# Order of the two weight halves, the engine of a small copy, and the place of the row sums in a two-layer decoder step

## The chip, the cores and the metric

The kernel runs on one core of one Trainium2 chip. The metric is the device time of one execution in microseconds. Before the change it is 1097.23 us, the median of three runs (1093.21, 1097.23 and 1097.97).

In the profile the engines are PE (TensorE, matmuls), PEld (its weight loads), DVE (VectorE), ACT (ScalarE), POOL (GpSimd) and SP (SyncE, which only issues transfers). L198 is line 198 of the kernel's file.

## What is computed

One inference step of a decoder with two layers: 512 new prompt tokens and 8 decode tokens, model width 1024, feed-forward width 2816, all in float32. Layer 0 mixes tokens by sliding-window attention with rotary positions, layer 1 by gated linear attention (GLA). Behind either stands a gated feed-forward block with a causal convolution of width 3 on its gate branch:

```python
def conv_ffn(x, buf, w_up, conv_w, conv_b, w_down):
    T = x.shape[1]
    h = x @ w_up
    a, u = h[..., :D_FF], h[..., D_FF:]
    ap = jnp.concatenate([buf.astype(a.dtype), a], axis=1)
    c = conv_b + sum(conv_w[j] * ap[:, j:j + T] for j in range(CONV_W))
    y = (jax.nn.gelu(c, approximate=False) * u) @ w_down
    return y, ap[:, T:]

# in each layer i, for the prompt and the decode tokens alike:
x = layer_norm(ALPHA * x + mixer(x), ln_mix_g[i], ln_mix_b[i])
f, conv = conv_ffn(x, buf, ffn_w_up[i], ffn_conv_w[i], ffn_conv_b[i], ffn_w_down[i])
x = layer_norm(ALPHA * x + f, ln_ffn_g[i], ln_ffn_b[i])
```

Outputs are the two activations, the key and value caches, the GLA states and the last two rows of each gate branch (the convolution's state).

## The kernel before

**Layout.** Activations are held transposed: 128 features on the partitions, tokens along the free dimension. The 520 tokens are cut into group a (256 prompt tokens) and group b (256 prompt tokens and the 8 decode tokens). A convolution runs along the free dimension, so group b needs the last two columns of group a: its history, kept in `hist`.

**Products in two parts.** TensorE is fed with `fp32r` values, a rounded float32. To keep accuracy every operand is split into a high part (rounded) and a low part (the rest): `wh`, `wl` for weights, `xh`, `xl` for activations. A product is high by high, high by low and low by high, three matmuls for each 128 by 128 block, all summed in PSUM. In `product` (L228 to L249) the matmuls with `wl` come last for some units (L247, `behind`).

**Weights.** The weights are cut into units of 128 by 1024 float32, 512 KB. Each unit is loaded by SP into one of two raw buffers (`raw`, L193), ScalarE or POOL rounds it into `wh`, and `wl` is made in one of two ways. In the first, VectorE subtracts (L204, L225, L318). In the second, which the program calls `low_by_dma` (L207 to L210), ScalarE writes the negated high part into `wl` and POOL issues a transfer that loads the same weight from HBM again and adds it to `wl` on the way: low = weight - high. The second way is used for the gate, value and down units of the feed-forward blocks, for the first weight block of each pair (below), and for the first units behind three of the four inner LayerNorms (`parts`, L212 to L226, whose operations are put behind chosen instructions of a LayerNorm).

**Stages of a layer.** The mixer and its output projection; the LayerNorm of group a, then that of group b (`ln_chunk`, `ln_end`); then the feed-forward block. Its 22 feature blocks run in two manners. The first four (`PAIRED`) are a gate unit and a value unit each, so eight units, multiplied for group a and group b separately (`ffn_gate`, `ffn_value`): the gate-and-value stage. The other 18 are pairs (`ffn_pair`), which multiply gate and value of both groups together with seven half products in place of eight, in the manner of Strassen and Winograd. For that they need sums and differences of rows of a and b, which `row_sums` (L460) and `row_sum1` (L505) make during the gate-and-value stage, with VectorE and ScalarE. Down projections are mixed in as soon as their inputs are there.

**The convolution's path in the gate-and-value stage** (L801 to L825). A tile `aext` gets two columns of history (zeros for group a, L807; a copy of `hist` for group b, L809) and the gate product behind them (L810). L812 to L814 apply the three taps, L816 saves the history of group a, L818 does the decode tokens with `base`, which POOL has worked out from the convolution's old state (`ffn_base`, L775 to L788: a transfer into `sconv` issued by ScalarE, then L783 to L787). GELU follows (L823), and the value unit's product is multiplied onto it (L831) and split.

**What sets the order.** Every engine and every transfer queue works in order. The program is written as generators: a counter `slot` rises by one with every product of a group, and a piece of work that yields n is taken up again n slots later (`spawn`, `due`). This gives an order of writing; a scheduler with a timeline simulation of its own then sets each engine's final order, with dependencies, the order of writing as priority, and bounds such as `issue_after(x)`, which puts instructions behind x on their engine. `behind_chain` (L790) uses it to put extra work behind the newest GELU and product. The row sums are spawned at the end of group b's LayerNorm (L450) and run in four parts: differences of the first half of the rows (L476, L478), then after 2, 3 and 2 further slots the other sums. The base is spawned 3 slots after the stage opens (L773).

```python
    def low_by_dma(self, l, h, src):
        self.nc.scalar.activation(l, h.bitcast(F32), AF.Copy, scale=-1.0)
        self.nc.gpsimd.dma_start(out=l, in_=src, accum_op=ALU.add)
```

Of the kernel before, what the change touches and what calls it, by code (L numbers as in the profile page):

```python
# [11 lines left out]
F32 = mybir.dt.float32  # L12
F32R = mybir.dt.float32r
I32 = mybir.dt.int32
AF = mybir.ActivationFunctionType
ALU = mybir.AluOpType
# [50 lines left out]
HEAVY = 2, 3, 5  # L67
# [35 lines left out]
class Net:  # L103
# [80 lines left out]
    def load_unit(self, u, pieces=1, late=False):  # L184
        src, nt = self.units[u][0], self.units[u][1]
        nc = self.nc
        if nt == 0:
            return self.load_rank(u)
        r = self.raw.tile([P, KD * P], F32, name="raw")
        h, l = ((self.wx if u == self.extra else self.wts).tile([P, KD * P], F32R, name=name) for name in ("wh", "wl"))  # L190
        n = nt * P // pieces
        for c in (slice(i * n, (i + 1) * n) for i in range(pieces)):
            nc.sync.dma_start(out=r[:, c], in_=src[:, c])  # L193
            if late:
                self.spawn(self.parts(u, h[:, c], l[:, c], r[:, c], src[:, c]), 1)
                continue
            if u >= HIACT:
                nc.scalar.activation(h[:, c], r[:, c], AF.Copy)  # L198
            else:
                nc.gpsimd.tensor_scalar(h[:, c], r[:, c], 1.0, 0.0, op0=ALU.mult, op1=ALU.add)  # L200
            if self.units[u][2] in (self.ffn_down2, self.ffn_gate, self.ffn_value):
                self.low_by_dma(l[:, c], h[:, c], src[:, c])
            else:
                nc.vector.tensor_tensor(l[:, c], r[:, c], h[:, c].bitcast(F32), op=ALU.subtract)  # L204
        self.w[u] = (h, l)

    def low_by_dma(self, l, h, src):  # L207

        self.nc.scalar.activation(l, h.bitcast(F32), AF.Copy, scale=-1.0)  # L209
        self.nc.gpsimd.dma_start(out=l, in_=src, accum_op=ALU.add)  # L210

    def parts(self, u, h, l, r, src):  # L212
# [5 lines left out]
        n = u - norm[4] if norm else 0  # L218
        with behind(norm and (*[norm[1]] * 4, self.square, self.exp)[n]):
            self.nc.scalar.activation(h, r, AF.Copy)  # L220
            if norm and self.phases.index(norm[4] - 1) in HEAVY:
                self.low_by_dma(l, h, src)
                return
# [31 lines left out]
    def pair_tasks(self, u):  # L255
# [13 lines left out]
        def upper():  # L269
# [3 lines left out]
            nc.sync.dma_start(out=r1, in_=src1)  # L273
            h, l = slot()
            nc.scalar.activation(h, r0, AF.Copy)
            self.low_by_dma(l, h, src0)
            keep(h, l, "a11", "a12")
# [99 lines left out]
    def ln_end(self, g, i, last=False):  # L377
# [70 lines left out]
        if i % 2 == 0:  # L448
            if g.i:
                self.spawn(self.row_sums(i), 1)  # L450
            return
# [8 lines left out]
    def row_sums(self, i):  # L460
# [13 lines left out]
        self.t1 = [self.ln.tile([P, NT - 256], F32, name=name, bufs=c)[:, :256] for name, c in (("sq", 2), ("sq", 2), ("mu", 1), ("msq", 1))]  # L474
        with self.tc.issue_after(self.rest):
            v.tensor_tensor(self.t1[0], row(a, 0), row(b, 0), op=ALU.subtract)  # L476
        for k in range(1, half):
            v.tensor_tensor(self.t1[k], row(a, k), row(b, k), op=ALU.subtract)  # L478
        yield 2
        with self.behind_chain():  # L480
# [11 lines left out]
            for k in range(half):  # L492
                v.scalar_tensor_tensor(tl[:, k], even(r)[:, k], -1.0, th[:, k].bitcast(F32), op0=ALU.mult, op1=ALU.subtract)
        yield 3
        with self.behind_chain():
# [305 lines left out]
    def ffn_gate(self, g, u, layer, j, q):  # L801
# [4 lines left out]
        if g.i == 0:  # L806
            nc.gpsimd.memset(a[:, 0:2], 0.0)  # L807
        else:
            self.pcopy(a[:, 0:2], self.hist[:, j])  # L809
        nc.scalar.copy(a[:, 2:2 + n], ps)  # L810
# [715 lines left out]
```

## Time and profile before

| | us |
|---|---|
| median of three runs | 1097.23 |
| the profiled execution | 1098.08 |
| its span, first to last instruction | 1096.1 |
| TensorE busy | 1058.4 (97%) |
| VectorE busy | 866.2 (79%) |
| ScalarE busy | 686.1 (63%) |
| GpSimd busy | 325.8 (30%) |
| granted TensorE clock, mean | 0.994 |

All times within the profile are counted from the start of the span. A row of a timeline has the start, the duration, the engine, the line, the operation, the tiles written and read, and in brackets the idle time of the engine before it with what ended it. The list of waits gives for each waiting line and releaser the total, the number and the longest. The granted clock is the share of full speed that TensorE was given. Transfers appear as issues, with the time from issue to landing.

### The profile page before, as it was taken

The numbers are of one execution on the slowest core, as the hardware profiler recorded it, in microseconds if no ns is written. First come the engines' busy times: TensorE is split into PE (matmuls) and PEld (weight loads), VectorE is DVE, ScalarE is ACT, GpSimd is POOL, SyncE is SP. The second block draws the span as 40 slices with busy tenths as digits, with TensorE's granted clock in tenths as the row PEclk, the third lists the DMA queues.
The fourth block names the chain that finished last, engine by engine and source line by source line (L and its number), as shares of the span: only waits on it lengthen the run. The fifth ranks groups of instructions, "written<-read, shape, count | busy, mean of one in ns | idle before, by whom it ended". The sixth has DMA issues, their size and how long they took to land.

```text
span 1096.1 us, 23852 instructions
## 1 busy us (share of the span) xinstructions
PE 1058.4 (97%) x9174; PEld 1029.8 (94%) x9174; DVE 866.2 (79%) x1812; ACT 686.1 (63%) x1356; POOL 325.8 (30%) x513
## 2 busy tenths in 40 slices
PE   8999999999999999999999999999899999999995
PEld 7998799999999999999999999898899999999995
DVE  7897758987788778978766767687888788778975
ACT  5677657776656665647666756477676656665643
POOL 3476553511111110274231111363311111110263
PEclk9999999999999999999999999999999999999998
DMA  6554139597777774348134455367487777774422
GB/s 228 150 162 136 24 108 226 129 221 183 181 174 175 174 190 117 111 144 220 55 115 157 132 157 172 93 173 209 127 212 187 181 173 177 174 188 117 114 68 79
DMA packets 65473, 167.44 MB, mean 153 GB/s; under 512 B 8104, under 2 KB 28624, under 8 KB 65360
## 3 DMA queue, kind: packets, MB, share of 16 engines
q1 hardware_dynamic: 50960, 119.47, 33.6%
q0 software_dynamic: 12240, 44.57, 23.2%
q10 hardware_dynamic: 2160, 1.89, 0.5%
q8 instruction: 72, 1.18, 0.4%
q14 instruction: 41, 0.34, 0.1%
HBM read 153.24 MB, written 8.47 MB: 148 GB/s over the span
## 4 chain that ended last, share of the span: by engine, by line
PE 76%; DVE 8%; DMA 6%; ACT 4%; POOL 2%; issue 2%; SPq 1%; DVEq 0%; ACTq 0%; POOLq 0%
PE widep L312 9%; PE widep L314 9%; PE widep L313 9%; PE accp L240 8%; PE accp L242 8%; PE accp L244 7%; PE widep L937 5%; PE widep L934 5%; PE widep L936 5%; DMA raw<-in_w_up 2%; PE accp L954 2%; DMA raw<-in_w_qkv 2%; PE onep L314 1%; PE onep L313 1%; PE onep L312 1%
## 5 line engine op out<-in xcount | busy, mean ns | idle before, releaser
L317 ACT ACTIVATE wh<-raw 128x1024 fp32r<-128x1024 f32 x72 | 76.3, 1060 | 96.2 <-PE widep L937 49.9
L198 ACT ACTIVATE wh<-raw 128x1024 fp32r<-128x1024 f32 (+1 forms) x91 | 95.0, 1047 | 40.7 <-PE widep L313 12.4
L313 PE MATMUL widep<-tl,wh 128*128 128x264 f32 (+1 forms) x432 | 119.1, 276 | 0.0
L314 PE MATMUL widep<-th,wl 128*128 128x264 f32 (+1 forms) x432 | 119.1, 276 | 0.0
L312 PE MATMUL widep<-th,wh 128*128 128x264 f32 (+1 forms) x432 | 119.1, 276 | 0.0
L240 PE MATMUL accp<-xh_b,wh 128*128 128x264 f32 x400 | 112.6, 282 | 2.5 <-DVE hprod L831 2.0
L244 PE MATMUL accp<-xh_b,wl 128*128 128x264 f32 x400 | 111.7, 280 | 0.0
L210 POOL DMA_DIRECT2D wl<-in_w_down x28 | 24.3, 866 | 284.2 <-ACT wl L209 273.1
L240 PE MATMUL accp<-xs_a,wh 128*128 128x256 f32 x400 | 105.6, 283 | 2.9 <-ACT wh L198 1.9
L242 PE MATMUL accp<-xl_b,wh 128*128 128x264 f32 x384 | 106.8, 278 | 0.0
L242 PE MATMUL accp<-xs_a,wh 128*128 128x256 f32 x384 | 102.1, 282 | 0.5 <-DVE xs_a L318 0.4
L318 DVE TENSOR_TENSOR wl<-raw,wh 128x1024 fp32r<-128x1024 f32 x72 | 88.1, 1223 | 8.1 <-ACT wh L317 8.1
L209 ACT ACTIVATE wl<-wh 128x1024 fp32r<-128x1024 f32 x85 | 89.3, 1053 | 1.1
L204 DVE TENSOR_TENSOR wl<-raw,wh 128x1024 fp32r<-128x1024 f32 (+2 forms) x63 | 77.9, 1244 | 14.0 <-ACT wh L198 13.4
L312 PEld LDWEIGHTS widep<-th,wh 128*128 128x128 f32 x432 | 82.1, 190 | 0.0
L313 PEld LDWEIGHTS widep<-tl,wh 128*128 128x128 f32 x432 | 82.1, 190 | 0.0
L314 PEld LDWEIGHTS widep<-th,wl 128*128 128x128 f32 x432 | 82.1, 190 | 0.0
L858 DVE TENSOR_TENSOR merged<-widep,conv 128x528 f32<-128x528 f32 x72 | 37.4, 561 | 55.3 <-PE widep L314 55.2
L240 PEld LDWEIGHTS accp<-xs_a,wh 128*128 128x128 f32 x400 | 76.4, 194 | 4.5 <-ACT wh L198 2.5
L312 PE MATMUL widep<-xh_b,wh 128*128 128x264 f32 x288 | 79.6, 276 | 0.0
L313 PE MATMUL widep<-xl_b,wh 128*128 128x264 f32 x288 | 79.5, 276 | 0.0
L314 PE MATMUL widep<-xh_b,wl 128*128 128x264 f32 x288 | 79.5, 276 | 0.0
(426 smaller groups left out, 4048.1 us busy)
## 6 DMA issues: line engine op xcount, KB each, us to landing
raw<-in_w_up SPq DMA_DIRECT2D x88, 512.0 KB, 3.9
wl<-in_w_up POOLq DMA_DIRECT2D x52, 512.0 KB, 6.6
raw<-in_w_down SPq DMA_DIRECT2D x44, 512.0 KB, 3.6
wl<-in_w_down POOLq DMA_DIRECT2D x28, 512.0 KB, 6.4
raw<-in_w_gla SPq DMA_DIRECT2D x24, 512.0 KB, 3.5
raw<-in_w_mix_o SPq DMA_DIRECT2D x16, 512.0 KB, 4.1
qs<-hl SPq DMA_DIRECT2D x64, 64.0 KB, 2.1
sgla<-in_state_gla SPq DMA_DIRECT2D x16, 256.0 KB, 2.7
```

Of the source, the lines that this page charges most:

```text
L198: nc.scalar.activation(h[:, c], r[:, c], AF.Copy)
L204: nc.vector.tensor_tensor(l[:, c], r[:, c], h[:, c].bitcast(F32), op=ALU.subtract)
L209: self.nc.scalar.activation(l, h.bitcast(F32), AF.Copy, scale=-1.0)
L240: nc.tensor.matmul(o, h[:, ks], xh, start=k == 0, stop=False)
L242: nc.tensor.matmul(o, h[:, ks], xl, start=False, stop=False)
L244: nc.tensor.matmul(o, l[:, ks], xh, start=False, stop=not tail and k == nt - 1)
L312: self.nc.tensor.matmul(o, h[:, ks], rh, start=k == 0, stop=False)
L313: self.nc.tensor.matmul(o, h[:, ks], rl, start=False, stop=False)
L314: self.final = self.nc.tensor.matmul(o, l[:, ks], rh, start=False, stop=k == KD // 2 - 1).ins
L317: self.nc.scalar.activation(hi, src, AF.Copy)
L318: self.nc.vector.tensor_tensor(lo, src, hi.bitcast(F32), op=ALU.subtract)
L934: self.final = nc.tensor.matmul(o, l[:, ks], rh, start=False, stop=k == nk - 1).ins
```

## The change

Three edits, all on how and when things are done; what is computed stays the same.

First, where the low part comes by an adding transfer, ScalarE writes the negated value straight from the raw weight (the rounding happens on writing), and this and the transfer stand before the copy that makes the high part. Before, the high part was made first and negated after. The number of operations and transfers is the same.

Second, group b's two columns of history are copied into `aext` by ScalarE in place of POOL.

Third, the row sums are spawned 4 slots after group b's LayerNorm in place of 1; all four first differences now stand behind the newest GELU and product (before, only the first was bound, behind the last low part of the LayerNorm), and the later parts follow after 1, 2 and 2 slots in place of 2, 3 and 2. So the four parts come at slots 4, 5, 7 and 9 in place of 1, 3, 6 and 8.

```diff
             if late:
                 self.spawn(self.parts(u, h[:, c], l[:, c], r[:, c], src[:, c]), 1)
                 continue
+            adding = self.units[u][2] in (self.ffn_down2, self.ffn_gate, self.ffn_value)
+            if adding:
+                self.low_by_dma(l[:, c], r[:, c], src[:, c])
             if u >= HIACT:
                 nc.scalar.activation(h[:, c], r[:, c], AF.Copy)
             else:
                 nc.gpsimd.tensor_scalar(h[:, c], r[:, c], 1.0, 0.0, op0=ALU.mult, op1=ALU.add)
-            if self.units[u][2] in (self.ffn_down2, self.ffn_gate, self.ffn_value):
-                self.low_by_dma(l[:, c], h[:, c], src[:, c])
-            else:
+            if not adding:
                 nc.vector.tensor_tensor(l[:, c], r[:, c], h[:, c].bitcast(F32), op=ALU.subtract)
...
-    def low_by_dma(self, l, h, src):
-
-        self.nc.scalar.activation(l, h.bitcast(F32), AF.Copy, scale=-1.0)
+    def low_by_dma(self, l, r, src):
+
+        self.nc.scalar.activation(l, r, AF.Copy, scale=-1.0)
         self.nc.gpsimd.dma_start(out=l, in_=src, accum_op=ALU.add)
...
         with behind(norm and (*[norm[1]] * 4, self.square, self.exp)[n]):
+            adding = norm and self.phases.index(norm[4] - 1) in HEAVY
+            if adding:
+                self.low_by_dma(l, r, src)
             self.nc.scalar.activation(h, r, AF.Copy)
-            if norm and self.phases.index(norm[4] - 1) in HEAVY:
-                self.low_by_dma(l, h, src)
+            if adding:
                 return
...
             h, l = slot()
+            self.low_by_dma(l, r0, src0)
             nc.scalar.activation(h, r0, AF.Copy)
-            self.low_by_dma(l, h, src0)
             keep(h, l, "a11", "a12")
...
             if g.i:
-                self.spawn(self.row_sums(i), 1)
+                self.spawn(self.row_sums(i), 4)
             return
...
-        with self.tc.issue_after(self.rest):
-            v.tensor_tensor(self.t1[0], row(a, 0), row(b, 0), op=ALU.subtract)
-        for k in range(1, half):
-            v.tensor_tensor(self.t1[k], row(a, k), row(b, k), op=ALU.subtract)
-        yield 2
+        with self.behind_chain():
+            for k in range(half):
+                v.tensor_tensor(self.t1[k], row(a, k), row(b, k), op=ALU.subtract)
+        yield 1
...
-        yield 3
+        yield 2
...
         else:
-            self.pcopy(a[:, 0:2], self.hist[:, j])
+            nc.scalar.copy(a[:, 0:2], self.hist[:, j])
         nc.scalar.copy(a[:, 2:2 + n], ps)
```

## The prediction

> **What bounds the kernel now.** I read the page first, then the waits of TensorE, then the chain of work that ended last, and only then single engines in time.
>
> ```profile
> PE 1058.4 (97%) x9174; PEld 1029.8 (94%) x9174; DVE 866.2 (79%) x1812; ACT 686.1 (63%) x1356; POOL 325.8 (30%) x513
> ```
>
> TensorE is busy for 1058.4 of 1096.1 us, so everything that a change of order can win lies in 38 us of gaps, and only those in the stages that the diff touches count. The waits of TensorE in the two gate-and-value stages (the window 168 to 217 us in the first layer, 739 to 792 us in the second) are these; columns: total, times, longest.
>
> ```profile
> PE accp L240 <- DVE hprod L831: 1.0, 1, 1.0
> PE accp L247 <- DMA wl<-in_w_up: 0.8, 1, 0.8
> PE accp L244 <- DMA wl<-in_w_up: 0.6, 1, 0.6
> PE accp L247 <- DVE xl_b L444: 0.4, 1, 0.4
> ...
> PE accp L244 <- DMA wl<-in_w_up: 3.4, 1, 3.4
> PE accp L247 <- DMA wl<-in_w_up: 1.3, 2, 1.0
> PE accp L240 <- DVE hprod L831: 1.0, 1, 1.0
> PE accp L247 <- DVE xl_b L444: 0.3, 1, 0.3
> ```
>
> That is 2.8 us in the first layer and 6.0 us in the second. The two stages run the same program, yet the second lasts 4 us longer (53 against 49 us), and the waits explain only 3.2 of them. The clock explains the rest (columns: window, us, PE, PEld, DVE, ACT, POOL busy with counts, granted clock, DMA share, GB/s):
>
> ```profile
> 776.90:780.20 3.30, 3.27 (x15) 3.27 (x16) 0.64 (x1) 1.10 (x2) 0.86 (x1) 0.50 0.17 15
> 203.20:206.50 3.30, 3.28 (x29) 3.28 (x30) 3.30 (x8) 2.78 (x5) 1.01 (x1) 1.00 0.00 0
> ```
>
> Right behind the 3.4 us wait the granted clock is 0.50 for 3.3 us: 15 matmuls where the same place of the first layer does 29. The 14 missing ones, at 3.3/29 us each, are 1.6 us. No shorter wait of this trace is followed by it. [...]
>
> What releases the wait at 203.2 us is told by the chain of the first layer (start, us, what):
>
> ```profile
> 169.84 8.80 DMA raw<-in_w_up
> ...
> 180.46 0.95 ACT wl L209
> ...
> 187.30 3.37 DMA sconv<-in_state_conv
> ...
> 190.75 3.29 POOL base L783
> ...
> 196.66 0.48 POOL base L786
> ...
> 197.43 0.31 POOL hist L321
> 197.74 5.44 DMA wl<-in_w_up
> 203.22 0.38 PE accp L244
> ```
>
> The accumulating transfer of the stage's last (eighth) unit is issued by POOL, in order, behind the convolution base and four small operations; it takes 5.44 us, and TensorE stands until it lands. In the second layer POOL's order has one more operation in front, the copy of the history that the diff moves to ScalarE (timeline of POOL; the bracket is idle time before):
>
> ```profile
> 761.75 3.13 POOL L783 TENSOR_TENSOR base<-sconv,par 128x176 f32<-128x176 f32 x1 [4.44 <-DMA sconv<-in_state_conv]
> ...
> 767.49 0.49 POOL L786 TENSOR_TENSOR base<-base,par 128x176 f32<-128x176 f32 x1
> ...
> 769.84 1.81 POOL L321 COPY aext<-hist 128x2 f32<-128x2 f32 x1 [1.21 <-DVE tl L318]
> 771.60 0.87 POOL L210 DMA_DIRECT2D wl<-in_w_up  x1
> ...
> 776.93 0.58 PE L244 MATMUL accp<-xs_a,wl 128*128 128x256 f32 x1 [3.43 <-DMA wl<-in_w_up]
> ```
>
> POOL waits 1.21 us for VectorE and then 1.81 us in the copy, with a ready transfer queued behind. So the two ends of the gate-and-value stages are set by when POOL issues this one transfer.
>
> **The change part by part.** *Negated part first.* ScalarE does the same two operations per weight in the other order, so no work is added. For the last unit:
>
> ```profile
> 193.41 1.06 ACT L198 ACTIVATE wh<-raw 128x1024 fp32r<-128x1024 f32 x1
> ...
> 195.96 1.08 ACT L209 ACTIVATE wl<-wh 128x1024 fp32r<-128x1024 f32 x1
> ```
>
> The negation can run where the copy ran and end by 194.47 instead of 197.04 us. POOL is in the base until 197.14 us, so the transfer can be issued right behind L786, ahead of the small operations: 197.74 - 197.14 = 0.60 us sooner. The high part comes one operation (1.06 us) later, and the raw buffer is free as much later; TensorE works on seven units before it and the wait list has none for a high part in these stages. That delay is hidden by products; uncovered it is 1.06 us per unit.
>
> *History on ScalarE.* It removes four POOL copies per layer and adds four to ScalarE. The nearest row for one there is another small copy:
>
> ```profile
> L872 ACT COPY merged<-widep 128x8 f32<-128x8 f32 x36 | 5.9, 163 | 37.3 <-DVE merged L858 37.3
> ```
>
> 163 ns, so 0.65 us per layer on an engine that is busy 63%; the bounds are 0 and 0.65 us, and I take 0. The new wait is that ScalarE now waits for POOL's copy into the history, with L810, L812 and the next GELU queued behind it; for three of the four gates that copy is long done, for the fourth it follows the base by well under 1 us and is needed several products later. In the second layer the removal lets the transfer go at the end of L786, 767.98, instead of 771.60 us: 3.62 us.
>
> *The base itself.* It starts when `sconv` lands, and that hangs on the same raw loads and ScalarE operations (169.84 to 187.30 us in the chain), since group b's LayerNorm waits behind them. In the new order an accumulate precedes a raw load in the transfers, and the table load follows two adjoining operations. A gain of one operation, 1.06 us, is the upper bound; the raw load issued one operation later gives -1.06 us as the lower. I take +0.5 us in each layer, because the chain holds the negation (0.95 us) between the raw load and the GELU, and accumulates that have been issued early leave less in front of `sconv`.
>
> *Row sums three units later.* Their first part's four subtractions, two small ones and four L489 (some 3.5 us) share VectorE with group b's low parts; the window is full:
>
> ```profile
> 187.10:195.40 8.30, 6.74 (x55) 6.16 (x54) 8.30 (x25) 4.09 (x10) 4.65 (x2) 1.00 0.27 65
> ...
> 204.00:217.00 13.00, 13.00 (x118) 13.00 (x117) 13.00 (x28) 11.57 (x19) 6.00 (x9) 1.00 0.54 136
> ```
>
> Put behind the low parts and the product, they no longer delay either: the waits on L444 and L831 go (1.4 and 1.3 us). This and the 0.8 and 1.3 us of earlier accumulates bring TensorE to the last unit sooner: without any of the waits listed, at 203.22 - 2.8 = 200.4 and 776.93 - 6.0 = 770.9 us. But there it waits: it goes on at 203.22 - 0.60 - 0.5 = 202.1 and 776.93 - 3.62 - 0.5 = 772.8 us. So these parts are worth nothing of their own while the base is the later one; they are cover for small new delays ahead (1.7 and 1.9 us).
>
> *Elsewhere.* The pair phases and the gated linear attention get the same swap. No TensorE wait names a weight of theirs, and raw loads there mostly wait for VectorE, not for the high part:
>
> ```profile
> SPq L273 <- DVE wl L318: 279.6, 30, 11.4
> ...
> SPq L193 <- ACT wh L198: 51.9, 25, 2.4
> ```
>
> So 0, hidden by the products of the pair before; 1.06 us per unit if not.
>
> **The sum.** 0.60 + 0.5 in the first layer, 3.62 + 0.5 in the second, and 1.6 us of clock, since the wait left there is 772.8 - 770.9 = 1.9 us: 6.8 us. The profiled execution took 1098.08 us (span 1096.1 and 2.0 around it), 0.85 above the median of 1097.23. Off its own time this gives 1091.3, off the median 1090.4; I forecast **1091.0 us**.
>
> **The rivals.** *All waits of the two stages go* (POOL takes the transfer between the base's operations, behind L783 at 194.04 us). Then TensorE's own arrival decides: 2.8 + 6.0 + 1.6 = 10.4 us, 1087 us. For it: the negation can be done at 194.47 us. Against it: in both layers POOL took the transfer only behind all of the base's operations.
>
> *The last transfer keeps its place* (the change doesn't do what it is for). POOL's order may still put it behind a copy that waits for VectorE. With only the 1.81 us copy gone it lands at 775.1 us, while TensorE arrives at 770.9: the wait is 4.2 us, the clock still falls, and the gain is 1.8 us or a little less: 1095.5 us.
>
> *The pairs start too early for VectorE.* The rows of the split that the first pair needs, and its matmul:
>
> ```profile
> 218.18 0.45 DVE L318 TENSOR_TENSOR xl_b<-msq,xh_b 128x256 fp32r<-128x256 f32 x1
> ...
> 221.95 0.28 PE L312 MATMUL widep<-xh_b,wh 128*128 128x264 f32 x1
> ```
>
> The slack is 3.3 us. VectorE is full from 204 to 217 us, so if the 3.5 us of row sums are not done before the base (where VectorE waits for POOL) but after it, the split ends at 222.1 us while the matmul wants it at 220.9: 1.2 us lost in the first layer, and by the same slack up to 5.9 in the second, where TensorE comes 5.7 us sooner. With 3 to 5.9 us lost there, 2.6 us of gain to 0.3 of loss are left, 1094.5 to 1097.5 us. Against it: they become due before the base is done.
>
> *Slower: raw loads behind accumulates starve ScalarE.* ScalarE's order holds a raw-dependent operation ahead of group a's normalised rows:
>
> ```profile
> 159.55 1.99 ACT L220 ACTIVATE wh<-raw 128x1024 fp32r<-128x1024 f32 x2
> 161.44 1.99 ACT L209 ACTIVATE wl<-wh 128x1024 fp32r<-128x1024 f32 x2
> ...
> 164.22 1.06 ACT L220 ACTIVATE wh<-raw 128x1024 fp32r<-128x1024 f32 x1 [0.47 <-DMA raw<-in_w_up]
> 165.18 1.80 ACT L443 ACTIVATE xs_a<-x_a,par 128x256 fp32r<-128x256 f32 x4
> ...
> 168.09 0.27 PE L240 MATMUL accp<-xs_a,wh 128*128 128x256 f32 x1
> ...
> raw<-in_w_up SPq DMA_DIRECT2D x1, 512.0 KB, 3.5
> ...
> raw<-in_w_up SPq DMA_DIRECT2D x1, 512.0 KB, 9.5
> ```
>
> The 3.5 us is the load issued at 160.62 us, with nothing ahead; the 9.5 us is one issued at 165.30 us behind two accumulates. With both negations first, the load goes up to 1.9 us later and takes 6.0 us longer, and a second raw operation stands before the rows: these start 9.0 us late, at 174.1, and TensorE stands from 168.09 to about 174.6 us, with the clock lost: 8.1 us. The old waits absorb 2.8 in the first layer and 7.6 in the second; 2 x 8.1 - 10.4 = 5.8 us slower, 1103 us. It decides from 5.2 us per layer on. Against it: if the order is negation, copy, negation, copy, only one accumulate is ahead, half the price, and below the bound; and ScalarE may take the rows first. [...]
>
> **How the numbers follow.** Forecast 0.50 (own range 1088.5 to 1093.5, from the bounds of the base's start, ±1.06 us twice, and the two ways to take off the sum), all waits gone 0.13, transfer keeps its place 0.20, pairs wait 0.09, slower 0.08. What a measurement of this kernel can tell from no change is about 0.5%, 5.5 us: faster is below 1091.7, slower above 1102.7. Two thirds of the forecast's case lie below 1091.7 (0.33); with all waits gone that makes 0.46. The rest of it, the third and the fourth case make 0.46 for the same. The range, 1086.5 to 1098.0, leaves out the slower case and the edge of the best one.
>
> **What would show it.** In the changed profile: the last accumulate of each stage issued right behind L786, with no history copy before it; the clock at 1.00 after 770 us; no wait on L444 or L831 in the two stages; a wait on `wl` of 1.5 to 2 us left in each. The forecast is wrong if the clock still falls, if a wait on `xs_a` appears at 168 or 739 us, or one at the first pair (217 to 222, 787 to 797 us), or if the base starts later than 190.75 us.

## The result, and the profile after

The changed kernel takes **1109.13 us** (median of 6 runs, 1101.13 to 1112.45) against 1097.12 for the kernel before on the same chip: a ratio of 1.0106, 95% interval 1.0079 to 1.0132. It is slower by 12 us where some 6 us of gain were forecast, and lies outside the forecast's range (1086.5 to 1098.0). The profiled execution took 1110.02 us, span 1108.0. First the busy line of its page, then TensorE's waits in the two gate-and-value stages, in two answers (the windows of the prediction, the second of which ends some 12 us ahead of the changed kernel's stage, with no wait in the rest; total, times, longest):

```profile
PE 1066.8 (96%) x9174; PEld 1037.2 (94%) x9174; DVE 868.9 (78%) x1812; ACT 687.2 (62%) x1364; POOL 309.6 (28%) x505
```

```profile
PE accp L247 <- DMA wl<-in_w_up: 4.2, 1, 4.2
PE accp L250 <- DMA wl<-in_w_up: 1.5, 1, 1.5
...
PE accp L247 <- DMA wl<-in_w_up: 3.0, 1, 3.0
PE tp L385 <- DVE s_a L377: 0.8, 1, 0.8
```

The waits for `hprod` (L831 before) have gone in both layers, as the edit was meant to do, and that for `xl_b` (L444 before) in the first; in the second 0.4 us of it is left. In their place stands one long wait in each layer for the eighth unit's low part. Both executions do the same 9174 matmuls, so the start of the n-th one in either trace (counted from 0, in us) tells where time went:

```
matmul    before     after     difference
 1560     196.64    196.97       0.33
 1620     204.22    210.50       6.28
 4380     515.40    522.68       7.28
 5100     603.36    614.47      11.11
 8880    1049.40   1061.61      12.21
```

Half of the loss arises within 60 matmuls at the end of the first layer's stage, 4 us in the gated linear attention, 1 us between the two, and 1 us in all that follows, the second layer's stage with it, where the wait of before (3.43 us, and the clock behind it) is only replaced by one of 3.0 and another stretch at half clock (granted clock 0.50 from 785.49 us). In the attention stand two waits, the first 1.0 us before and with a stretch at half clock behind it now (from 608.00 us), the second at a matmul that waited 0.4 us for another tile before. What delays these two stays open. The second is 1.5 us in e1, e7 and e11 below as well, which all swap the units behind the LayerNorms, but the first isn't tied to the swap: it is 2.5 us in e10, which swaps nothing.

```profile
PE tp L1236 <- DVE sg L1240: 1.9, 1, 1.9
...
PE accp L243 <- ACT msq L1226: 1.5, 1, 1.5
```

The chain of waits through the first layer's stage (start, us, what) shows what the long wait hangs on:

```profile
164.30 8.73 DMA raw<-in_w_up
...
175.14 7.95 DMA raw<-in_w_up
183.09 0.02 issue
183.11 1.07 ACT wl L210
...
189.61 3.81 DMA sconv<-in_state_conv
...
193.49 0.86 POOL base L785
...
198.03 0.50 POOL base L788
198.53 6.61 DMA wl<-in_w_up
...
205.19 0.58 PE accp L247
```

The accumulate is issued right behind the base, as forecast. But the base starts 2.74 us later than before (193.49 against 190.75), and the transfer takes 6.61 in place of 5.44 us. The base itself is 1.35 us shorter than before (5.04 against 6.39) and the place behind it saves the 0.60 us of the forecast, so the low part lands 1.96 us later (205.14 against 203.18). The matmul that waits for it is now number 1588, where it was number 1612: 24 matmuls, some 2.7 us, that filled TensorE's time before now stand behind the wait, and a stretch at half clock (from 205.22 us, some 1.6 us) follows it. These three make 6.26 of the 6.28 us. ScalarE's timeline at the start of the stage says why the base is late:

```profile
160.39 1.04 ACT L210 ACTIVATE wl<-raw 128x1024 fp32r<-128x1024 f32 x1
161.34 1.99 ACT L224 ACTIVATE wh<-raw 128x1024 fp32r<-128x1024 f32 x2
163.23 1.04 ACT L210 ACTIVATE wl<-raw 128x1024 fp32r<-128x1024 f32 x1
...
169.26 1.07 ACT L210 ACTIVATE wl<-raw 128x1024 fp32r<-128x1024 f32 x1 [2.10 <-DMA raw<-in_w_up]
...
173.11 1.06 ACT L210 ACTIVATE wl<-raw 128x1024 fp32r<-128x1024 f32 x1 [0.67 <-DMA raw<-in_w_up]
```

Before, the two copies that read the raw buffers ran first and the two negations read the high parts, so both buffers were free after the first 1.99 us. Now either buffer is free only after the second operation that reads it, at 162.3 and 164.3 us, and by then an accumulating transfer is under way. The second reload's 8.73 us stands in the chain, the first one's time to landing is in the list of transfers:

```profile
raw<-in_w_up SPq DMA_DIRECT2D x1, 512.0 KB, 6.8
```

Before, these took 3.5 and 5.1 us. ScalarE stands 2.10 us where it stood 0.47. The later loads of the stage queue behind accumulates in both kernels: four that can be followed take 6.3 to 9.5 us before and 6.4 to 8.2 us now.

### The profile page after: what moved, and what is told of

Read it like the earlier page. It is cut to its first block, busy times and chain, and to the rows that moved or that the text cites. A ratio compares the mean times of both kernels' runs of the same rounds, so it can differ in the third digit from the quotient of the medians.

```text
span 1108.0 us, 23884 instructions
## 1 busy us (share of the span) xinstructions
PE 1066.8 (96%) x9174; PEld 1037.2 (94%) x9174; DVE 868.9 (78%) x1812; ACT 687.2 (62%) x1364; POOL 309.6 (28%) x505
## 4 chain that ended last, share of the span: by engine, by line
PE 73%; DMA 9%; DVE 7%; ACT 6%; issue 3%; POOL 2%; SPq 1%; DVEq 0%; ACTq 0%; POOLq 0%
PE widep L317 8%; PE widep L316 8%; PE widep L315 8%; PE accp L243 8%; PE accp L245 8%; PE accp L247 7%; PE widep L938 5%; PE widep L936 5%; PE widep L939 5%; DMA raw<-in_w_up 3%; DMA raw<-in_w_qkv 1%; DVE wl L205 1%; PE onep L317 1%; PE onep L316 1%; PE onep L315 1%
## 5 line engine op out<-in xcount | busy, mean ns | idle before, releaser
L243 PE MATMUL accp<-xs_a,wh 128*128 128x256 f32 x400 | 109.6, 291 | 4.0 <-ACT wh L201 2.0
L245 PE MATMUL accp<-xs_a,wh 128*128 128x256 f32 x384 | 104.9, 287 | 0.0
L210 ACT ACTIVATE wl<-raw 128x1024 fp32r<-128x1024 f32 x85 | 89.1, 1048 | 16.5 <-DMA raw<-in_w_up 13.9
L205 DVE TENSOR_TENSOR wl<-raw,wh 128x1024 fp32r<-128x1024 f32 (+2 forms) x63 | 77.7, 1240 | 13.5 <-ACT wh L201 13.4
L243 PEld LDWEIGHTS accp<-xs_a,wh 128*128 128x128 f32 x400 | 79.4, 199 | 6.6 <-ACT wh L201 2.6
L247 PE MATMUL accp<-xs_a,wl 128*128 128x256 f32 x256 | 74.1, 293 | 7.8 <-DMA wl<-in_w_up 7.2
```

Of the source, the lines that this page charges most:

```text
L210: self.nc.scalar.activation(l, r, AF.Copy, scale=-1.0)
L243: nc.tensor.matmul(o, h[:, ks], xh, start=k == 0, stop=False)
L245: nc.tensor.matmul(o, h[:, ks], xl, start=False, stop=False)
L247: nc.tensor.matmul(o, l[:, ks], xh, start=False, stop=not tail and k == nt - 1)
```

## The experiments

The expectations name theories by number or letter. The first three are: the swap delays the raw loads (1, later A); the other two edits are to blame (2); it is only chance where the clock falls (3). The kernel before was run again on the same chip beside each group of runs, so between groups ratios are compared and not microseconds. Of each edit only the telling lines are shown.

**One edit at a time.** The kernel before with single edits of the diff.

```diff
# e1: the change's hunks with low_by_dma only
-                self.low_by_dma(l[:, c], h[:, c], src[:, c])
+                self.low_by_dma(l[:, c], r[:, c], src[:, c])
# e4, and e2 together with e3's
-            self.pcopy(a[:, 0:2], self.hist[:, j])
+            nc.scalar.copy(a[:, 0:2], self.hist[:, j])
# e3: all of the row sums' hunks, and e2
-                self.spawn(self.row_sums(i), 1)
+                self.spawn(self.row_sums(i), 4)
```

> The kernel before with the first edit alone: the negated value first, from the raw weight, at all three places; history copy and row sums as before. Theory 1 (the swap delays the raw loads: in the changed kernel ScalarE does wl, wh, wh, wl at 160 us, the raw loads land 5 to 6 us later and behind accumulates, sconv lands at 193.4 in place of 190.67 us, the base ends at 198.6 in place of 197.1, and the last accumulate lands at 205.1 in place of 203.2): this kernel has the loss nearly whole, 1105 to 1112 us, with raw loads landing at about 169 and 173 us, idle time of some 2 us on ScalarE behind a raw load, sconv behind 192 us, and the wait at the last unit of layer 0 at 4 us or more. Theory 2 (it is the row sums' later place or the history copy that pushes the order about, and the swap alone brings the accumulate forward): 1091 to 1096 us, sconv by 190.7 us. Theory 3 (only the clock: the loss is the number of 3.4 us stretches at half clock times 1.6 us, by chance of where they fall): within 3 us of before, and the difference is 1.6 us per stretch.

> The kernel before with the second and third edit alone (history copied by ScalarE, row sums three units later), without the swap. Theory 1: none of the loss; the wait of 3.43 us at 776.9 us shrinks because POOL's 1.81 us copy and its 1.21 us wait are gone from in front of the last accumulate, the waits for xl_b and hprod in the two stages go, and raw loads land as before (164.1, 166.7 us): 1089 to 1094 us. Theory 2: this kernel has the loss, 1104 to 1111 us, with sconv landing after 192 us. Theory 3: within 3 us of before.

> The kernel before with the third edit alone, the row sums three units later. Theory 1: the 2.7 us of waits for xl_b and hprod in the two stages go, but TensorE then waits as much longer for the last accumulate, so no change: 1095 to 1098 us. Theory 2: loss of 5 us or more: above 1102 us. Theory 3: within 3 us of before.

> The kernel before with the second edit alone, the history copied by ScalarE. Theory 1: POOL issues the last accumulate of layer 1 some 3.6 us sooner (768 in place of 771.6 us), the wait of 3.43 us goes or falls below 1 us and the clock with it: a gain of 3 to 5 us, 1092 to 1094 us, and layer 0 as before. Theory 2 (ScalarE stands at the copy until POOL has written the history, with the next gate's product and GELU behind it): 1099 us or more. Theory 3: within 3 us of before.

Measured: e1 1105.16 us (ratio 1.0085, interval 1.0053 to 1.0118), e2 1093.12 (0.9955, 0.9934 to 0.9976), e3 **1091.06** (0.9943, 0.9923 to 0.9963), e4 1093.13 (0.9965, 0.9947 to 0.9983). The swap is the loss; the other edits gain, and theories 2 and 3 fall. Two expectations missed. e1 has no long wait at the first layer's eighth unit (its base starts at 192.8 us, its accumulate lands at 201.5): TensorE was held up ahead of it by 1.68 us for `hprod` and came after the landing. In the profiles, of the 8.9 us that e1 has lost by the end of the second layer's stage, only 2 had arisen by the end of the first layer's, and 3 arise in the attention. And e3 alone gains 6 us where nothing was expected. POOL's timeline of e3, in the first layer and then in the second, shows a part of why:

```profile
190.64 0.49 POOL L782 TENSOR_TENSOR base<-sconv,par 128x176 f32<-128x176 f32 x1 [5.30 <-DMA sconv<-in_state_conv]
191.09 0.67 POOL L783 TENSOR_TENSOR hprod<-sconv,par 128x176 f32<-128x176 f32 x1
...
193.03 0.55 POOL L785 TENSOR_TENSOR base<-base,par 128x176 f32<-128x176 f32 x1
...
759.66 1.33 POOL L782 TENSOR_TENSOR base<-sconv,par 128x176 f32<-128x176 f32 x1 [3.81 <-DMA sconv<-in_state_conv]
...
767.63 0.25 POOL L321 COPY aext<-hist 128x2 f32<-128x2 f32 x1 [1.56 <-DVE conv L813]
768.59 0.88 POOL L210 DMA_DIRECT2D wl<-in_w_up  x1 [0.71 <-ACT wl L209]
```

In the first layer the base starts when it did before, but ends at 193.58 in place of 197.14 us: 2.94 us long, not 6.39. Other VectorE work lies beside it (see the last section). By the starts of matmuls, though, some 5 of the 6 us arise in the second layer's stage, and there the base is only 0.66 us shorter (5.57 us). It starts 2.09 us sooner, the history copy takes 0.25 in place of 1.81 us, and so the accumulate goes at 768.59 in place of 771.60 us. TensorE's order has moved too: 39 matmuls of group b, not 24, now stand ahead of the 22 that need the low part. The 3.43 us wait is 0.24 us in e3, and the stretch at half clock behind it has gone: the matmuls there start 0.11 us apart, those of before 0.21. Over the whole execution the mean granted clock of e3 is 0.993 all the same, against 0.994 before. How much each of these is worth was not separated.

**Buffer or order of the halves?** The changed kernel with the two things that the swap does taken apart.

```diff
# e5, in all three places: high part first, both from raw
+            nc.scalar.activation(h, r, AF.Copy)
             self.low_by_dma(l, r, src)
-            nc.scalar.activation(h, r, AF.Copy)
# e6: negation first, high part from it
         nc.scalar.activation(l, r, AF.Copy, scale=-1.0)
+        nc.scalar.activation(h, l.bitcast(F32), AF.Copy, scale=-1.0)
         nc.gpsimd.dma_start(out=l, in_=src, accum_op=ALU.add)
```

> The changed kernel, but with the high part first and the negation second, both read from the raw weight. So the high part is as early as in the kernel before, while the raw buffer is still freed only by the second of the two operations, as in the changed kernel. Theory A (the loss is the raw buffer: its next load is issued only with or behind the accumulating transfer of the same unit and lands behind it): the loss stays, 1103 to 1112 us, raw loads of layer 0's stage land at 168 us and later and ScalarE stands some 2 us for them. Theory B (the loss is that every high part comes one operation later): no loss, 1090 to 1095 us.

> The changed kernel, but the high part is made from the negated part (scale -1) in place of from the raw weight; the transfer follows both. So the negation is first and the high part one operation late, as in the changed kernel, while the raw buffer is freed by the first operation, as in the kernel before. Theory A: no loss; raw loads land as before (about 164 and 167 us), sconv by 191 us, 1088 to 1095 us. Theory B: the loss stays, 1103 to 1112 us.

Measured: e5 1108.82 us (1.0124, 1.0100 to 1.0148), e6 1092.11 (0.9960, 0.9947 to 0.9972). Theory A holds in both, theory B fails in both: which half comes first is worth nothing, and the kernel whose first operation frees the raw buffer is 1.6% faster. Not all of the 1.6% is the raw loads: TensorE's order at the eighth unit differs between the two as well (the table below), which the later runs put at 0.5 to 0.7%. ScalarE's wait for a raw load in e5, then in e6:

```profile
173.86 1.06 ACT L222 ACTIVATE wh<-raw 128x1024 fp32r<-128x1024 f32 x1 [2.92 <-DMA raw<-in_w_up]
```

```profile
164.44 1.06 ACT L210 ACTIVATE wl<-raw 128x1024 fp32r<-128x1024 f32 x1 [0.44 <-DMA raw<-in_w_up]
```

**Why the edits don't add up, and the eighth unit by itself.**

```diff
# e7: e1's and e3's hunks
# e8: e3's hunks, and in load_unit, ahead of the copy into h
+            last = any(u == e + 7 for e in (self.phases[2], self.phases[5]))
+            if last:
+                self.low_by_dma(l[:, c], r[:, c], src[:, c])
```

> The kernel before with the first and third edit (swap and later row sums), the history still copied by POOL. The swap alone cost 8.0 us, the row sums alone gained 6.0, the history copy alone 4.0, and all three together cost 12.0, so something works against itself. Theory C (the swap moves the base 2 to 3 us later, and the row sums, moved later too, now stand beside it on VectorE: the base, 3.1 us long in the swap alone at 192.8 us, becomes 5 us long, its accumulate issues at 198.5 in place of 195.9 us, and TensorE waits 3.5 us or more): the pair alone already shows it, 1106 to 1111 us. Theory D (the third party, ScalarE's history copy, is what hurts in company): 1098 to 1103 us, base 3.1 us long, accumulate issued by 196 us.

> The kernel before with the row sums later, and the swap only for the eighth unit of each gate-and-value stage, the one whose accumulate stands behind the base; all other units high part first. Theory A: the raw loads keep their times (164 to 167 us), the last accumulate can go right behind the base (at 193.6 us in place of 195.84 us with the row sums alone); TensorE waited only 0.2 to 0.4 us for it there, so the gain over the row sums alone is at most 0.6 us: 1089.5 to 1092 us. If already this one swap delays loads (the next raw load, of the first down unit, then follows the accumulate): 1093 us or more.

Measured: e7 1105.48 us (1.0097, 1.0067 to 1.0126). Neither theory: the base is 2.98 us long, not 5 (against C), yet the 6 us of the row sums are gone (D's upper edge is passed). By the intervals e1, e7 and the changed kernel can't be told apart, so the order "8.0 less 6.0 less 4.0 gives 12.0" needs no story of three parties, only a reason why the gains vanish beside the swap. e8 gave one: 1097.77 us (1.0024, 1.0007 to 1.0041), 0.8% more than e3 for one unit's swap in each layer, where at most 0.6 us of gain was expected. The accumulate's issue, the wait, and the transfers' times to landing, in e3 and then in e8:

```profile
195.84 0.88 POOL L210 DMA_DIRECT2D wl<-in_w_up  x1 [0.99 <-ACT wl L209]
...
201.42 0.38 PE L244 MATMUL accp<-xs_a,wl 128*128 128x256 f32 x1 [0.15 <-DMA wl<-in_w_up]
```

```profile
193.10 0.87 POOL L215 DMA_DIRECT2D wl<-in_w_up  x1
...
201.10 0.58 PE L249 MATMUL accp<-xs_a,wl 128*128 128x256 f32 x1 [3.54 <-DMA wl<-in_w_up]
...
wl<-in_w_up POOLq DMA_DIRECT2D x1, 512.0 KB, 8.0
raw<-in_w_down SPq DMA_DIRECT2D x1, 512.0 KB, 5.0
```

Issued 2.74 us sooner, the transfer lands 0.3 us sooner: it now runs beside the raw load of the first down unit and takes 8.0 in place of 5.5 us. And TensorE is there 3.5 us too soon, because its order has changed. The order of its matmuls around the eighth unit of the first layer, read from the traces (a: group a's product of that unit, b: group b's products):

```
before, e2, e3, e4; swap of the six units (e11) or the pairs (e12)   a2  b24  a22
e6                                                                   a2  b15  a22
changed kernel, e1, e5, e7, e8                                       a24
```

In the second layer the number of b between a2 and a22 is 24 before, in e4 and e11, 39 in e2, e3 and e12, 20 in e6, 6 in e5 and 3 in the changed kernel and e7; e1 and e8 have a24. The kernel's scheduler has a timeline of its own. Where the accumulate stood behind the base, it held back the 22 matmuls from the first one that needs the low part and put a product of group b in front. With the swap it pulls them 24 matmuls, 2.7 us, forward (21 in the second layer of the changed kernel), and the transfer doesn't follow. That it does so because its timeline has the transfer issued early is argued from the program; no run shows that timeline. It costs only where TensorE is there ahead of the transfer: from matmul 1560 to 1620 e1 and e7, with a24 as well, take 6.7 and 8.6 us, the kernel before 7.6 and the changed kernel 13.5.

**Putting the product back, and the swap's other places.** In e9 and e10 the eighth unit's product of group a is written one product of group b later.

```diff
# e9 is e8, e10 is e3, with this in order()
+                eighth = u == p0 + 7 and p0 in (self.phases[2], self.phases[5])
-                if not joint:
+                if not joint and not eighth:
                     out.append((0, u))
                 while b <= u - max(lead, 1):
                     out.append((1, b))
                     b += 1
+                if eighth:
+                    out.append((0, u))
# e11: e3 and the swap's hunk in parts; e12: e3 and its hunk in the pairs
```

> The kernel with the later row sums and the swap of the eighth unit alone, which took 1097.8 us against 1091.1 with the row sums alone, and in addition the eighth unit's product of group a written one product of group b (24 matmuls) later. In the row sums alone, as in the kernel before, TensorE's order there is 2 matmuls of this product, 24 of group b, then the other 22; with the swap the scheduler gave all 24 in one piece, 22 of them before those of group b. Theory E (the accumulate lands no sooner, 201.06 against 201.38 us, and the loss is that the scheduler moved the product 24 matmuls, 2.7 us, forward to meet it): with the product put back the wait of 3.5 us in the first layer and 4.1 in the second falls to below 1.5 us each and the clock stays up there: 1090 to 1093 us. Theory F (the loss is in the transfer itself, 7.96 us beside the down unit's raw load, and whoever waits for that load): the loss stays, 1096 to 1099 us.

> The control for the run before: later row sums and the eighth unit's product written one product of group b later, no swap anywhere. By either theory as with the row sums alone, 1090 to 1092.5 us.

> Later row sums, and the swap only for the six units behind the LayerNorms (three places: both gate-and-value stages and the start of the gated linear attention); the first and eighth unit, the down units and the pairs keep the high part first. TensorE's order at the eighth unit is then that of the kernel before (2, 24 and 22 matmuls). Theory A (raw buffer freed late): raw loads land at 168 us and later, the base starts 2 to 3 us late, and the attention's start loses 1 to 3 us more: 1096 to 1104 us. If the whole loss were the order at the eighth unit (theory E alone): 1090 to 1093 us.

> Later row sums, and the swap only in the 36 pairs. TensorE never waited for a weight there and the pairs' raw loads mostly wait for VectorE: no change against the row sums alone, 1090 to 1092.5 us. If the later free raw buffer counts there too (one operation of 1.06 us for each of 36 pairs at most): up to 1100 us, with waits of TensorE named after the pairs' weights.

Measured: e9 1091.43 us (0.9952, 0.9935 to 0.9970), e10 1092.95 (0.9974, 0.9957 to 0.9992), e11 1102.99 (1.0067, 1.0042 to 1.0092), e12 1092.69 (0.9965, 0.9945 to 0.9985). By its time theory E holds: with the product put back the loss of e8 is gone (how far the traces bear this out is said with e16). e10, the control, lies 0.45 us above its range, e12 0.2. Against e3 the pairs' swap is worth 0.2% at most, within the intervals. The six units behind each LayerNorm cost 1.2% although TensorE's order at the eighth unit is that of before, so they are a cause of their own. In e11 the accumulate of the eighth unit ends up last of all, behind a history copy that takes 3.61 us (POOL's timeline, then TensorE's):

```profile
191.26 3.61 POOL L323 COPY aext<-hist 128x2 f32<-128x2 f32 x1 [1.22 <-DVE conv L815]
194.82 0.49 POOL L784 TENSOR_TENSOR base<-sconv,par 128x176 f32<-128x176 f32 x1
...
203.18 0.87 POOL L210 DMA_DIRECT2D wl<-in_w_up  x1
```

```profile
208.51 0.38 PE L246 MATMUL accp<-xs_a,wl 128*128 128x256 f32 x1 [2.11 <-DMA wl<-in_w_up]
```

**Do the two causes add up, and which half of the delay is it?**

```diff
# e13: the changed kernel with e9's hunk in order()
# e14: the changed kernel, with this in parts (e15: e6 likewise)
-                self.low_by_dma(l, r, src)
+                self.nc.scalar.activation(l, r, AF.Copy, scale=-1.0)
```

e14 and e15 leave out the adding transfers of the six units, and e16 is e9 once more, for another profile.

> The changed kernel, all three edits, with the eighth unit's product of group a written one product of group b later (as the run before did for the swap of that unit alone). If the two causes add up, this takes the order's share away and leaves the raw loads' share: 1101 to 1105 us, with raw loads of layer 0 still landing at 169 us and later, and the waits of 4.21 and 3.00 us for the eighth unit's transfer below 1.5 us. If one of them covers the other: 1107 to 1112 us (order worth nothing while the raw loads are late).

> The changed kernel without the adding transfers of the six units behind each LayerNorm; their low part is left as the negated high part, so that part of the computation is left out, and so is 3 MB of loading in each of the three places. The raw buffers are still freed by the second operation. If the raw loads are late mainly because they run behind an accumulating transfer: they now land 3.5 to 4 us after their issue (in the changed kernel 6.8 and 8.7 us), ScalarE waits below 1 us for them, and this kernel is within 2 us of the next one. If mainly because they are issued late: 4 us or more slower than the next one, with ScalarE's waits as before.

> The same without the adding transfers, but with the raw buffer freed by the first operation (negation from the raw weight, high part from the negated one); the same part of the computation is left out. 1084 to 1093 us by either theory: no accumulating transfer in front of the raw loads, and raw loads early.

> The kernel of the earlier run (later row sums, swap of the eighth unit alone, its product one product of group b later), once more for its profile: again 1090 to 1093 us, the accumulate issued right behind the base at about 193 us, landing near 201 us, and a wait of TensorE for it below 1.5 us in each layer.

Measured: e13 1100.59 us (1.0053, 1.0029 to 1.0076), e14 1096.37 (1.0019, 0.9995 to 1.0043), e15 1086.86 (0.9928, 0.9911 to 0.9945), e16 1092.31 (0.9960, 0.9940 to 0.9980). The causes add up, as far as the intervals tell: e13 lies 0.4 us below the range for this. From matmul 1560 to 1620 it takes 7.4 us. TensorE's waits in e13, first and second layer:

```profile
PE accp L250 <- DMA wl<-in_w_up: 2.0, 1, 2.0
...
PE accp L247 <- DMA wl<-in_w_up: 0.7, 1, 0.7
```

The waits of 4.2 and 3.0 us at the eighth unit are 0 and 0.7; the 2.0 us is an earlier unit's low part, late with its raw load. e14 settled half of its question. Without the accumulates the raw loads land 3.5 us after issue although issued late (seven loads, median), and ScalarE doesn't wait for one in this stage; its load of the convolution's state is issued at 185.76 us against 185.41 in e15:

```profile
raw<-in_w_up SPq DMA_DIRECT2D x7, 512.0 KB, 3.5
```

So the late release costs the base only 0.35 us by itself; the delay of 2 to 3 us is the queueing behind accumulates. Nevertheless e14 is 9.5 us slower than e15, where 2 us were expected. TensorE's waits in e14 (over the whole execution) have those for the two eighth units' low parts and one in the attention at their head:

```profile
PE accp L247 <- DMA wl<-in_w_up: 6.2, 2, 3.1
PE accp L243 <- ACT z_b L1032: 2.1, 1, 2.1
```

By the starts of matmuls, 4.3 and 3.6 us of the difference arise at the two eighth units, which fits TensorE's order (a24 in e14, a2 b15 a22 in e15), and the mean granted clock is 0.990 in e14 against 0.994 in e15; the pair was not run with the product put back. Another 3.5 us arise at the start of the attention, with the wait of 2.1 us for `z_b`, so there the late release, or what hangs on it, is not free; why was not followed.

e16 missed in one point, and it weakens theory E. In the first layer the wait is gone, with the accumulate in 5.3 us, and the matmuls 1560 to 1620 take 6.7 us less than in e8. In the second layer a wait stays, 4.06 us in e8 and 3.70 here, where the accumulate of 763.09 us was issued 0.19 us behind a down unit's raw load and took 8.4 us:

```profile
771.57 0.58 PE L249 MATMUL accp<-xs_a,wl 128*128 128x256 f32 x1 [3.70 <-DMA wl<-in_w_up]
```

In this trace the second layer's stage (matmuls 6300 to 6500) takes 4.6 us longer than in e3, and e16 comes out near e3 only because it was 3.8 us ahead by then, 2.7 of them by matmul 1400, early in the first layer's stage. So the order is shown to be the loss in the first layer; in the second layer putting it back did not help here, though in e13 that stage is 3.5 us shorter than in the changed kernel.

## Why the prediction was wrong, point by point

**"The base itself: +0.5 us."** This is the step that failed, with the wrong sign. Its lower bound, -1.06, priced a raw load issued one operation later and left out that the stage's first two reloads then land behind an accumulate (6.8 and 8.7 us where they took 3.5 and 5.1). The rows for it were quoted in the fourth rival: 3.5 us with nothing ahead, 9.5 behind two accumulates. The base came 2.74 us late in the first layer, which is the prediction's own sign of being wrong ("later than 190.75 us"). Removing the accumulates (e14) removes nearly all of that delay; freeing the buffer early (e6) removes the loss, together with more than half of the move in TensorE's order.

**The last accumulate.** Its place behind L786 was right (e8, the changed kernel). That it would land as much sooner as it is issued was wrong: 5.44 us was taken as fixed. It is 5.44 and 5.28 us before (first and second layer), 5.5 in e3 and 5.3 in e11 (first layer); with a raw load issued 0.30 us ahead and 0.01 us behind it is 6.61 and 6.77 in the changed kernel, and with one 0.19 us ahead 8.4 in e16 (second layer). In e16's first layer it is 5.3, and the raw load issued between 191 and 193 us, near the accumulate's 191.63, takes 6.8. The kernel before issued that raw load 3.24 us ahead of it; the change brings both together (198.23 and 198.53 us).

**"TensorE goes on at 202.1."** The sum moved the transfer and left TensorE's order as it was. The section on the kernel before says that a scheduler sets that order, and it moved by 24 matmuls. So TensorE went on at 205.19 us, and with 24 more matmuls still to do. This step appears nowhere in the prediction, in no rival, and costs 6 to 8 us: e8 less e9, 0.7%; the changed kernel less e13, 0.5%.

**The rival that came true in part** is the slower one: late raw loads, ScalarE idle. Its time was 1103 and its place was wrong. ScalarE took group a's rows first (the rival's own "against"), TensorE waited 0.3 us for them, and the loss came through the convolution's state, the base and the eighth unit. The rival has a reload take 6.0 us longer (9.5 less 3.5); the first one took 3.3 us longer (6.8 less 3.5). The next two loads in the chain (8.73 and 7.95 us) were each issued while the load ahead of it in the same queue was still under way, until 169.18 and 177.74 us, and of the 9.5 us of before 8.2 lie behind the landing of the load ahead of it. In the traces of before and after the transfers of one queue land in the order of their issue: all 203 of SP that can be followed, and all 85 of POOL.

**History on ScalarE: 3.62 us**: right, with some luck. Alone (e4) it gains 4.0 us, with the second layer's accumulate issued at 768.52 us (forecast 767.98) and no wait for a low part above 0.7 us, where one was 3.4. That the clock gave its 1.6 us there is not shown: the mean granted clock of e4 is 0.994, as before. Its base started 0.92 us later than before and was 1.5 us shorter, neither of which was forecast.

**Row sums: "worth nothing of their own".** Wrong: 6 us alone. The base and TensorE's order were taken as given, though in e3 the base is 3.4 us shorter in the first layer, starts 2.1 us sooner in the second, and 15 more matmuls fill the second layer's wait.

**"Elsewhere ... So 0."** Right for the pairs (e12), wrong for the gated linear attention, where the profile has 4 us of the 12. Of these 1.1 us are the longer wait for `msq`, which goes with the swap behind the LayerNorms; the rest is the wait for `sg` and the clock, whose cause stays open.

**The clock.** The forecast of one half-clock stretch less was wrong: ahead of the stretch at the end that both have, the profile of the changed kernel has four where that of before has one, some 1.6 us each. The first of them (136.96 us) lies ahead of the first weight whose halves change places (152.9 us). No run shows the 1.6 us of clock in the sum, the second layer's wait of 3.4 us cut to 1.9 with the clock kept up: the changed kernel has a wait of 3.0 us there and a fall behind it. Behind the gap of 1.92 us in the attention it fell, behind a wait of 1.59 us in e6 (to 202.93 us) it did not.

**The whole.** By ratios it splits into history and row sums -0.45% (e2), raw loads about +1.0% (e13 less e2) and TensorE's order +0.5% (the changed kernel less e13). Taken as such differences the parts make +1.06% by construction; measured apart, the order is 0.7% (e8 less e9) and the raw loads 1.2% (e11 less e3).

## What to carry over

Before an operation is put first because something waits for its result, ask which operation frees its input, and what the freed buffer's next load will queue behind; here two reads of one buffer in place of one turned two loads of 3.5 and 5.1 us into loads of 6.8 and 8.7. Where a scheduler sets the order, compare the resulting order on every engine, also on those that the edit doesn't touch. Of the kernels that compute everything, the later row sums alone (e3) have the lowest ratio, 0.57% below before, with e2, e6 and e9 within the intervals; so negation first is harmless if the high part is made from the negated one (e6).

## What was not expected of the hardware

**The clock fell also behind gaps shorter than its stretch of 3.41 us.** Granted clock and TensorE's busy time in the changed kernel, in pairs of windows ahead of and behind a fall:

```profile
133.55:136.96 3.41, 2.28 (x18) 1.99 (x18) 2.10 (x5) 1.34 (x5) 3.41 (x7) 1.00 0.00 0
136.96:140.37 3.41, 3.41 (x19) 3.17 (x19) 0.84 (x2) 0.00 (x0) 1.24 (x5) 0.50 0.01 2
201.81:205.22 3.41, 0.03 (x1) 0.04 (x1) 3.41 (x11) 0.99 (x5) 1.24 (x2) 1.00 0.75 136
205.22:208.63 3.41, 3.41 (x16) 3.41 (x17) 3.38 (x7) 3.31 (x5) 0.30 (x1) 0.50 0.00 0
604.58:608.00 3.42, 1.50 (x14) 1.28 (x12) 3.42 (x8) 0.64 (x2) 0.00 (x0) 1.00 0.65 208
608.00:611.40 3.40, 3.40 (x17) 3.31 (x16) 2.14 (x6) 3.16 (x8) 0.51 (x1) 0.50 0.92 275
```

The falls at 136.96, 205.22, 608.00 and 785.49 us lie whole multiples (20, 118 and 52) of 3.413 us apart, and each lasts one such stretch. TensorE was busy for 2.28 of the 3.41 us ahead of the first and 1.50 ahead of the third, whose gap was 1.92 us. In e11 the matmuls start 0.21 us apart from 209.84 us on, behind a wait of 2.11 us (to 208.51 us). Other short gaps have no fall behind them: in e6 the matmuls go on 0.11 us apart behind the wait of 1.59 us (to 202.93 us). TensorE's busy time alone is not the measure, since it is 1.95 us in the window 184.74 to 188.16 us of the changed kernel and 2.28, as in the first row above, in the window 135.07 to 138.48 us of the kernel before, and the granted clock is 1.00 in the stretch behind either. What the clock counts stays open.

**POOL's time for one operation differed with what VectorE did beside it.** The same product of 128x176 values took 3.29 us before (from 190.75 us) and 0.49 in e3 (from 190.64); copies of the two history columns took 0.19 to 3.61 us. VectorE's rows beside that product, before and then in e3:

```profile
190.46 1.35 DVE L444 SCALAR_TENSOR_TENSOR xl_b<-x_b,par,xh_b 128x264 fp32r<-128x264 f32 x3
191.70 0.51 DVE L489 SCALAR_TENSOR_TENSOR raw<-x_b,par,mu 128x256 f32<-128x256 f32 x1
```

```profile
190.48 0.41 DVE L830 TENSOR_TENSOR hprod<-conv,accp 128x256 f32<-128x256 f32 x1
190.81 1.24 DVE L477 TENSOR_TENSOR sq<-x_a,x_b 128x256 f32<-128x256 f32 x2
```

Before, one operation on two large SBUF tiles follows the other; in e3 most of the product lies beside L830, one of whose inputs, `accp`, is in PSUM. That the place of these tiles makes the factor of 6.7 between the two products (3.29 and 0.49 us) is the author's estimate from these rows; no run separates it. Which of the two engines gives way the rows don't settle: beside L477 in e3 POOL's next product took 0.67 us, and there VectorE's subtractions took up to 0.78 us, where those of the changed kernel take 0.42.
